# The first hidden tile of a streaming encoder: where ACT's squares, the norm row's copies and the first cached loads stand in their queues

## The chip, the cores and the metric

The kernel runs on one core of one Trainium2 chip. The metric is the device time of one execution in microseconds, the median over the runs shown. Traces come from the hardware profiler, one execution per kernel.

## What is computed

The reference is one inference step of a two-layer encoder for two groups of requests that share weights: a prompt group (512 new frames) and a sample group (64 frames of a running stream, with 1024 cached frames). Each layer is

```python
h = rmsnorm(x, norm_pre)                 # 1024 features per frame
cols_A, cols_B = split(h @ w_in)         # one combined input projection
x = x + rmsnorm(concat(silu(g_A) * A(h), silu(g_B) * B(h)) @ w_out, norm_post)
```

Layer 0 pairs multi-head latent attention (A) with stick-breaking attention (B); layer 1 pairs chunk-band attention with forgetting attention. The sample group's attention also reads cached keys and values. The change lies in the first microseconds of layer 0: `rmsnorm` of the input, its transposed copy, and the first 416 columns of `w_in` (the latents of A); and in the loads of the cached keys and values of B.

## The kernel before, in words

TensorE works in float32 split in two: every operand is kept as a rounded high part and a low part (the rest), and a product of two such operands is three matmuls (high x high, high x low, low x high).

The head of the kernel treats the input in five tiles: four of 128 prompt rows (tiles 0 to 3) and one of 64 sample rows (tile 4). Each tile is two halves of 512 features.

- `load_x` (L778) issues the two DMAs of a tile on SP's queue. `landed` (L159) makes a DMA wait, on its queue, until another DMA has landed; in the loop, tile 1's loads and the first two weight loads wait so for the first half of tile 0.
- `put_h` (L207) squares each half on ACT (L211, with the sum over the row read out), makes the reciprocal root on POOL (L197, L198), and scales the tile by it and by the norm row on DVE (L214).
- `put_hT` (L217) transposes a half with four PE transposes into one of two `psT` banks (L221), then ACT copies it as the high part of `hT` (L224) and DVE subtracts for the low part (L225).
- The norm row is one row of 1024 numbers. Two PE products with a column of ones spread it over 128 partitions into two `psA` banks (`nps`, L801). Tile 0 reads it there; ACT copies it into SBUF (`npre`, L809) for tiles 1 to 4.
- The weights of the first projection, eight slices k0 to k7 of 128 x 416, are loaded (`wraw`, four buffers), rounded to the high part on ACT (`chi`, L173), and their low part is made on POOL or, for k3 and k6, on DVE (L177). A load needs its `wraw` buffer back from the low part of the slice four before. In the loop, k0 and k1 follow tile 0; k2 to k5 tile 1; k6 and k7 tile 2.
- `tm_chunk` (L281) then makes the projection tile by tile: 24 matmuls of 128 x 128 by 416 columns into one of two `psA` banks (L270; L278 for the sample tile), three for each slice k, in the order k0 to k7. ACT copies the bank out (L854).
- After it come the pairs of heads of stick-breaking attention (`qk_pair`, L260 matmuls). `sb_sample` (L873) reads the cache in three chunks: `s_keys` (L530) loads 256 or 384 cached keys into `kraw` (two buffers) and `s_vals` (L544) the values into `vraw` (two buffers); ACT and POOL or DVE split them into high and low parts (L540, L541; L554, L555).

The order in which each engine and each queue gets its instructions isn't the program's: when the kernel is built, a planner simulates the engines and DMAs with estimated times, and at each moment gives a free engine the ready instruction of the best rank (program order, with a lead for the blocks under `tc.high_priority`). Each engine and each queue then runs its list strictly in that order on the chip. `tc.issue_after(ins)` makes the planner put the instructions of its block behind `ins` on `ins`'s engine, without a wait on a semaphore.

Of the kernel before, what the change touches and what calls it, by code (L numbers as in the profile page):

```python
# [1 line left out]

# [1 line left out]

# [9 lines left out]
AF = mybir.ActivationFunctionType  # L14
# [3 lines left out]
P = 128  # L18
# [41 lines left out]
def f32(ap):  # L60
    return ap.bitcast(F32)
# [3 lines left out]
def kernel(ctx: ExitStack, tc: tile.TileContext, a: dict, o: dict):  # L65
    nc = tc.nc
# [27 lines left out]
    def ring(shape, dt, tag, name=None):  # L94
        p, n = rings[tag]
        if isinstance(p, list):
            rings[tag][1] += 1
            return p[n % len(p)].tile(shape, dt, name=nm(name or tag), tag=tag, bufs=1)
        return p.tile(shape, dt, name=nm(name or tag), tag=tag, bufs=n)
# [4 lines left out]
    def Er(shape, name="e"):  # L104
        return ring(shape, F32, "E", name)
# [10 lines left out]
    def bank(tag, bufs, n=512):  # L116
        return lambda: pp.tile([P, n], F32, name=nm("ps" + tag), tag=tag, bufs=bufs)

    psA, psS, psT, psU, psX = bank("A", 2), bank("S", 2), bank("T", 2), bank("U", 1), bank("X", 1)
# [39 lines left out]
    def landed(dma, first):  # L159

        if first is not None:
            tc.add_manual_dep(dma.ins, first.ins.name,
                              mybir.DependencyInfo(mybir.DependencyClass.Sync, mybir.DependencyReason.DATA),
                              reason="landed")
        return dma
# [36 lines left out]
    ROOT = 1.0 / 32  # L202
# [1 line left out]
    def halves(x):  # L204
        return [x[:, :512], x[:, 512:]]

    def put_h(x, rows, npre, out):  # L207

        ss = St([P, 2])
        for c in range(2):  # L210
            nc.scalar.activation(psX()[:rows], x[c][:rows], AF.Square, scale=ROOT, accum_out=ss[:rows, c:c + 1])  # L211
        r = rstd_of2(ss, rows)
        for c in range(2):
            nc.vector.scalar_tensor_tensor(out=out[c][:rows], in0=x[c][:rows], scalar=r[:rows],  # L214
                                           in1=npre[c][:rows], op0=ALU.mult, op1=ALU.mult)

    def put_hT(x, rows, col, h):  # L217
        for g in range(2):
            t = psT().rearrange("p (a b) -> p a b", a=4)
            for k in range(4):  # L220
                nc.tensor.transpose(t[:, k, :rows], x[g][:rows, k * P:(k + 1) * P], ident[:rows, :rows])  # L221
            hi = h.m[g][:, :, 0, col:col + rows]
            lo = h.m[g][:, :, 1, col:col + rows]
            nc.scalar.copy(hi, t[:, :, :rows])  # L224
            nc.vector.tensor_sub(lo, t[:, :, :rows], f32(hi))  # L225
            if rows == DS:
                nc.vector.tensor_copy(out=h.s[g][:, :, 0:DS], in_=f32(hi))
                nc.vector.tensor_copy(out=h.s[g][:, :, DS:P], in_=f32(lo))

    def bcast(src_row, n):  # L230
        return bass.AP(src_row.tensor, src_row.offset, [[0, P], [1, n]])
# [78 lines left out]
    def drain():  # L310
        for _ in side[0]:
            pass
# [205 lines left out]
    def s_pv(po, ph, pl, vt, vnew, wd, first, last):  # L518
# [8 lines left out]
        for n, (l, r) in enumerate(ops):  # L527
            nc.tensor.matmul(po[:, :256], l, r, start=(first and n == 0), stop=(last and n == len(ops) - 1))  # L528

    def s_keys(kdram, c, new):  # L530

        k0, wd, nw = c
        raw = ring([P, 384], F32, "kraw")
        nc.sync.dma_start(raw[:, :wd], kdram[:, k0:k0 + wd])
        w = wd
        if nw:
            nc.gpsimd.tensor_copy(out=raw[:, wd:wd + nw], in_=new)
            w += nw
        kh, kl = ring([P, 384], F32R, "sK"), ring([P, 384], F32R, "sK")
        nc.scalar.copy(kh[:, :w], raw[:, :w])  # L540
        nc.gpsimd.tensor_sub(kl[:, :w], raw[:, :w], f32(kh[:, :w]))  # L541
        return kh, kl

    def s_vals(vdram, c, new):  # L544

        k0, wd, nw = c
        b0, nb = k0 // P, wd // P
        raw = ring([P, 3, P], F32, "vraw")
        nc.sync.dma_start(raw[:, :nb], vdram[:, b0:b0 + nb])
        v = ring([P, 3, 256], F32R, "vs")  # L550
        for dst, src in ((v[:, :nb], raw[:, :nb]),) + (((v[:DS, nb:nb + 1], new.unsqueeze(1)),) if nw else ()):
            src = src.rearrange("p a (s d) -> p a s d", s=2)
            hi = dst.rearrange("p a (s d) -> p a s d", s=4)[:, :, ::3, :]
            nc.scalar.copy(hi, src)  # L554
            nc.vector.tensor_sub(dst[:, :, 64:192].rearrange("p a (s d) -> p a s d", s=2), src, f32(hi))  # L555
        return v
# [217 lines left out]
    h0 = new_h(big)  # L774
# [3 lines left out]
    def load_x(t, first=None):  # L778
        rows = P if t < NT else DS
        x = [Rr([P, 512], "x") for _ in range(2)]  # L780
        ds = [landed(nc.sync.dma_start(f32(x[c][:rows]), xrow(t)[:, c * 512:(c + 1) * 512]), first) for c in range(2)]
        return [f32(y) for y in x], ds[0]
# [10 lines left out]
    x, first = load_x(0)  # L793
# [3 lines left out]
    nc.vector.memset(ones, 1.0)  # L797
    nps = []
    for c in range(2):
        nps.append(psA())  # L800
        nc.tensor.matmul(nps[c], ones, nrow[:, c * 512:(c + 1) * 512], start=True, stop=True)  # L801
    for t in range(NT + 1):
        rows = P if t < NT else DS
        put_h(x, rows, npre if t else nps, x)
        put_hT(x, rows, t * P, h0)
        if t == 0:
            npre = [Er([P, 512], "npre") for _ in range(2)]
            for c in range(2):
                nc.scalar.copy(npre[c], nps[c])  # L809

            nrm = Fr([P, 384], "nrm")
            for dst, src in ((rope, a["rope"]), (nrm[:, :256], bcast(a["a_q_norm"], 256)),
                             (nrm[:, 256:], bcast(a["a_kv_norm"], 128))):
                tc.keep_in_program_order(nc.scalar.dma_start(dst, src))
        if t < NT:
            c0_weights(C0W[t], first)
            x, _ = load_x(t + 1, first)
            first = None


# [74 lines left out]
    for p in range(NPAIR - 1):  # L895
        nxt = sb_qk(p + 1)
        if p == 1:
            v_chunk(sb, 1, a["w_vb"][1], h0, o["p_sbv"])
        if p == 1:
            tc.keep_in_program_order(nc.sync.dma_start(o["s_bandk"][:CL - DS], a["band_k"][DS:]))  # L900
            tc.keep_in_program_order(nc.sync.dma_start(o["s_bandv"][:CL - DS], a["band_vn"][DS:]))
        gate_tile(a["ws"][8 + p], h0, 4 + p, True)
        with tc.high_priority(PR_sb):
            beside(sb_sample(p), EV_sb)
            sb_pair(p, pr)
            drain()
        pr = nxt
    gate_tile(a["ws"][11], h0, 7, True)
    nc.sync.dma_start(o["s_sbv"], sb.vn)
# [179 lines left out]
    for c0 in range(0, PAST, 512):  # L1089
        raw = w_tile("wraw", [P, 512], F32)  # L1090
# [6 lines left out]
    t = psA()  # L1097
# [3 lines left out]
    for i in range(2):  # L1101
        raw = w_tile("wraw", [P, 512], F32)
# [6 lines left out]
    for i in range(2):  # L1109
        raw = w_tile("wraw", [P, 4, P], F32)  # L1110
# [68 lines left out]
    npre = l0.tile([P, D], F32, name="npre", tag="rq", bufs=1)  # L1179
# [164 lines left out]
    t = psT()  # L1344
    for i in range(NT):
        nc.tensor.transpose(t[:H, i * P:(i + 1) * P], lf[:, i, :], ident)
    c = Er([P, S], "cum")
# [3 lines left out]
    for k in range(3):  # L1351
        c = Er([P, 384], "cum")
# [3 lines left out]
    t = psT()  # L1356
# [191 lines left out]
```

## Time and profile before

| | |
|---|---|
| median of 3 runs | 833.12 us (832.88 to 835.7) |
| the profiled execution's own time | 829.8 us |
| its span, first to last instruction | 827.9 us |
| PE busy | 766.3 us (93% of the span), 5581 instructions |
| DVE, ACT, POOL busy | 507.6, 499.2, 382.6 us (61%, 60%, 46%) |
| the chain that ended last | PE 70%, DVE 10%, ACT 7%, DMA 5%, issue 4%, POOL 4% |
| DMA | 95.52 MB, mean 115 GB/s |

A busy time is the sum of an engine's instructions; matmuls overlap, so a busy PE isn't PE at its peak. The chain is followed back from the last instruction, at each step to what released it. In a timeline row the first number is the start in microseconds from the span's start, the second how long the merged instructions took, and the bracket at the end how long the engine was idle before, and what released it. "SPq" is SP's queue of DMA issues.

### The profile page before, as it was taken

Reading aid. Unit: us, or ns where it says so; the run is one execution under the profiler, and the core shown is the slowest. Engines: PE = TensorE matmul, PEld = TensorE weight load, DVE = VectorE, ACT = ScalarE, POOL = GpSimd, SP = SyncE. Lnnn points to the kernel's source line nnn. Section 1 sums busy time; section 2 is a strip of 40 time slices with the busy share of each in tenths; the row PEclk is TensorE's granted clock in tenths of the full one; section 3 lists DMA queues with packets and bytes.
Section 4 is the critical chain, followed back from the end, with each engine's and each line's share of the span. In section 5 each row is a group of like instructions: output and inputs, shape, how many; then the busy total and the mean of one; then the engine's idle time right before and its main releaser. Section 6 shows DMA issues by size and latency. Waiting matters only on the chain.

```text
span 827.9 us, 16285 instructions
## 1 busy us (share of the span) xinstructions
PE 766.3 (93%) x5581; PEld 713.1 (86%) x5581; DVE 507.6 (61%) x1318; ACT 499.2 (60%) x1342; POOL 382.6 (46%) x461
## 2 busy tenths in 40 slices
PE   6989999999997999989868999999997999999986
PEld 4989899989895888788767999999897899998986
DVE  4544765777847675738962654664754576658345
ACT  7554664776747675666542755575644767768521
POOL 7584342654427131055772644553344444546453
PEclk9999999999999999999998999999999999999999
DMA  8243324441123022146352443433223543551562
GB/s 271 60 145 114 101 73 146 142 122 53 54 68 109 29 73 74 40 139 218 122 171 72 123 118 104 136 110 99 87 81 111 170 127 111 158 140 55 158 228 102
DMA packets 69924, 95.52 MB, mean 115 GB/s; under 512 B 9529, under 2 KB 40489, under 8 KB 69810
## 3 DMA queue, kind: packets, MB, share of 16 engines
q1 hardware_dynamic: 69264, 94.12, 37.7%
q8 instruction: 44, 0.72, 0.4%
q14 instruction: 38, 0.31, 0.2%
q10 hardware_dynamic: 578, 0.37, 0.1%
HBM read 74.36 MB, written 18.79 MB: 113 GB/s over the span
## 4 chain that ended last, share of the span: by engine, by line
PE 70%; DVE 10%; ACT 7%; DMA 5%; issue 4%; POOL 4%; SPq 1%; DVEq 0%; POOLq 0%; ACTq 0%
PE psA L260 27%; PE psA L270 15%; PE psU L435 5%; PE psX L528 4%; PE psT L426 4%; PE psA L278 3%; PE psS L563 2%; PE psS L460 2%; PE psS L461 2%; POOL m L751 1%; DMA part<-part 1%; PE psT L509 1%; ACT whi L173 1%; DMA x<-in_x_prompt_dram 1%; PE psA L989 1%
## 5 line engine op out<-in xcount | busy, mean ns | idle before, releaser
L260 PE MATMUL psA<-hT,whi 128*128 128x320 f32 (+1 forms) x1216 | 258.5, 301 | 3.8 <-DVE foxqbl L353 2.0
L177 POOL TENSOR_TENSOR wlo<-wraw,whi 128x512 fp32r<-128x512 f32 (+2 forms) x130 | 168.6, 1307 | 188.4 <-ACT whi L173 146.2
L260 PEld LDWEIGHTS psA<-hT,whi 128*128 128x128 f32 x1216 | 198.8, 190 | 6.8 <-issue 2.7
L260 PE MATMUL psA<-hT,wlo 128*128 128x320 f32 (+1 forms) x608 | 183.5, 302 | 0.0
L270 PE MATMUL psA<-whi,hT 128*128 128x256 f32 (+2 forms) x812 | 162.8, 287 | 6.8 <-DVE m L745 5.5
L270 PEld LDWEIGHTS psA<-whi,hT 128*128 128x128 f32 x812 | 130.0, 188 | 9.5 <-DVE m L745 6.4
L270 PE MATMUL psA<-wlo,hT 128*128 128x256 f32 (+2 forms) x420 | 121.2, 288 | 0.0
L260 PEld LDWEIGHTS psA<-hT,wlo 128*128 128x128 f32 x608 | 115.8, 190 | 0.8
L173 ACT CAST whi<-wraw 128x512 fp32r<-128x512 f32 (+2 forms) x130 | 78.2, 616 | 39.8 <-PE psA L260 21.4
L270 PEld LDWEIGHTS psA<-wlo,hT 128*128 128x128 f32 x420 | 79.5, 189 | 0.8
L371 POOL TENSOR_TENSOR kz<-kf,r 64x256 fp32r<-64x256 f32 x48 | 36.7, 765 | 30.5 <-ACT kf L365 28.8
L430 DVE TENSOR_TENSOR pt1l<-psT,pt1h 128x384 fp32r<-128x384 f32 x64 | 39.6, 620 | 14.6 <-ACT pt1h L429 13.7
L1237 DVE CUSTOM_DVE_ANT_0 x<-psS,T 128x128 f32<-128x128 f32 (+1 forms) x64 | 31.0, 484 | 23.0 <-PE psT L426 8.5
L447 POOL TENSOR_TENSOR g<-g,oT 128x512 f32<-128x512 f32 x14 | 18.3, 1304 | 53.8 <-DVE oT L439 53.5
L541 POOL TENSOR_TENSOR sK<-kraw,sK 128x384 fp32r<-128x384 f32 (+2 forms) x32 | 30.3, 946 | 26.3 <-ACT sK L540 24.6
L469 ACT ACTIVATE psS<-x,st 128x128 f32<-128x128 f32 (+1 forms) x64 | 34.1, 532 | 13.8 <-DVE st L1237 13.5
L429 ACT CAST pt1h<-psT 128x384 fp32r<-128x384 f32 x64 | 33.9, 531 | 12.6 <-PE psT L426 11.7
L528 PE MATMUL psX<-vs,sP 128*128 128x256 f32 (+1 forms) x184 | 38.6, 303 | 1.5 <-DVE sP L515 1.2
L439 DVE SCALAR_TENSOR_TENSOR oT<-psU,oT 64x256 f32<-64x256 f32 x64 | 26.8, 419 | 18.6 <-ACT oT L438 17.7
L460 PE MATMUL psS<-r,r 128*128 128x256 f32 (+1 forms) x96 | 35.4, 370 | 2.6 <-DVE st L1237 1.7
L347 ACT ACTIVATE r<-psA 64x256 fp32r<-64x256 f32 x48 | 18.2, 378 | 32.4 <-PE psA L260 16.9
L472 DVE TENSOR_SCALAR x<-psS,st 128x128 f32<-128x128 f32 (+1 forms) x64 | 35.1, 548 | 1.3
(390 smaller groups left out, 1893.9 us busy)
## 6 DMA issues: line engine op xcount, KB each, us to landing
wraw<-in_ws_dram SPq DMA_DIRECT2D x80, 256.0 KB
wraw<-in_w_out_dram SPq DMA_DIRECT2D x32, 256.0 KB
x<-in_x_prompt_dram SPq DMA_DIRECT2D x16, 256.0 KB
part<-part SPq DMA_DIRECT2D x32, 128.0 KB
m<-part SPq DMA_DIRECT2D x16, 256.0 KB
r<-r SPq DMA_DIRECT2D x48, 64.0 KB
out_dram<-kout SPq DMA_DIRECT2D x12, 256.0 KB
out_dram<-vf SPq DMA_DIRECT2D x24, 128.0 KB
```

The lines of the kernel that those rows point to most:

```text
L173: nc.scalar.copy(hi, raw)
L177: eng.tensor_sub(lo, raw, f32(hi))
L260: nc.tensor.matmul(ps[:, :c1 - c0], w[:, k % 4, :], h.m[k // 4][:, k % 4, x, c0:c1], start=(k == 0 and n == 0), stop=(k == KT - 1 and n == 2))
L270: nc.tensor.matmul(ps[:, :n], h.m[k // 4][:, k % 4, x, t * P:(t + 1) * P], w[:, k % kp, :], start=(k == ks[0] and m == 0), stop=(k == ks[- ...
L371: nc.gpsimd.tensor_sub(pair.kl[s][me, cs], kf[me, cs], f32(k[me, cs]))
L429: nc.scalar.copy(ph[:, :i + 1, at], tv)
L430: nc.vector.tensor_sub(pl[:, :i + 1, at], tv, f32(ph[:, :i + 1, at]))
L435: nc.tensor.matmul(po, m.v[p // 2, j][:, p % 2, s * P:(s + 1) * P], x[:, j, :], start=(j == 0 and x is ph), stop=(j == 2 * hq + 1 and x is ...
L460: nc.tensor.matmul(ps[:, :w], pair.qq[s][:, q], pair.kk[s][:, :w], start=True, stop=False)
L469: nc.scalar.activation(ps[:, :n], src, AF.Exp, bias=mn, scale=-1.0, accum_out=sm)
L472: nc.vector.tensor_scalar(out=w[:, :n], in0=ps[:, :n], scalar1=rs, scalar2=None, op0=ALU.mult)
L528: nc.tensor.matmul(po[:, :256], l, r, start=(first and n == 0), stop=(last and n == len(ops) - 1))
```

## The change

Three edits. The norm row's two products go to `psS` banks and no longer to `psA`. On ACT, the squares of tile 1 and the two copies of the norm row are put behind the last transposed copy of tile 0 (the second half's L224). The DMAs of cached keys and values of the first pair of heads (`lead[0]` is set while the head runs and cleared after the first pair's pass) wait on SP's queue until the first half of the input tile loaded last, the sample tile, has landed.

```diff
--- before.py
+++ after.py
@@ -1,4 +1,4 @@
-from contextlib import ExitStack
+from contextlib import ExitStack, nullcontext
 
 import numpy as np
 
@@ -204,11 +204,12 @@
     def halves(x):
         return [x[:, :512], x[:, 512:]]
 
-    def put_h(x, rows, npre, out):
+    def put_h(x, rows, npre, out, behind=None):
 
         ss = St([P, 2])
-        for c in range(2):
-            nc.scalar.activation(psX()[:rows], x[c][:rows], AF.Square, scale=ROOT, accum_out=ss[:rows, c:c + 1])
+        with tc.issue_after(behind.ins) if behind else nullcontext():
+            for c in range(2):
+                nc.scalar.activation(psX()[:rows], x[c][:rows], AF.Square, scale=ROOT, accum_out=ss[:rows, c:c + 1])
         r = rstd_of2(ss, rows)
         for c in range(2):
             nc.vector.scalar_tensor_tensor(out=out[c][:rows], in0=x[c][:rows], scalar=r[:rows],
@@ -221,11 +222,12 @@
                 nc.tensor.transpose(t[:, k, :rows], x[g][:rows, k * P:(k + 1) * P], ident[:rows, :rows])
             hi = h.m[g][:, :, 0, col:col + rows]
             lo = h.m[g][:, :, 1, col:col + rows]
-            nc.scalar.copy(hi, t[:, :, :rows])
+            done = nc.scalar.copy(hi, t[:, :, :rows])
             nc.vector.tensor_sub(lo, t[:, :, :rows], f32(hi))
             if rows == DS:
                 nc.vector.tensor_copy(out=h.s[g][:, :, 0:DS], in_=f32(hi))
                 nc.vector.tensor_copy(out=h.s[g][:, :, DS:P], in_=f32(lo))
+        return done
 
     def bcast(src_row, n):
         return bass.AP(src_row.tensor, src_row.offset, [[0, P], [1, n]])
@@ -527,11 +529,13 @@
         for n, (l, r) in enumerate(ops):
             nc.tensor.matmul(po[:, :256], l, r, start=(first and n == 0), stop=(last and n == len(ops) - 1))
 
+    lead = [None]
+
     def s_keys(kdram, c, new):
 
         k0, wd, nw = c
         raw = ring([P, 384], F32, "kraw")
-        nc.sync.dma_start(raw[:, :wd], kdram[:, k0:k0 + wd])
+        landed(nc.sync.dma_start(raw[:, :wd], kdram[:, k0:k0 + wd]), lead[0])
         w = wd
         if nw:
             nc.gpsimd.tensor_copy(out=raw[:, wd:wd + nw], in_=new)
@@ -546,7 +550,7 @@
         k0, wd, nw = c
         b0, nb = k0 // P, wd // P
         raw = ring([P, 3, P], F32, "vraw")
-        nc.sync.dma_start(raw[:, :nb], vdram[:, b0:b0 + nb])
+        landed(nc.sync.dma_start(raw[:, :nb], vdram[:, b0:b0 + nb]), lead[0])
         v = ring([P, 3, 256], F32R, "vs")
         for dst, src in ((v[:, :nb], raw[:, :nb]),) + (((v[:DS, nb:nb + 1], new.unsqueeze(1)),) if nw else ()):
             src = src.rearrange("p a (s d) -> p a s d", s=2)
@@ -797,16 +801,18 @@
     nc.vector.memset(ones, 1.0)
     nps = []
     for c in range(2):
-        nps.append(psA())
+        nps.append(psS())
         nc.tensor.matmul(nps[c], ones, nrow[:, c * 512:(c + 1) * 512], start=True, stop=True)
     for t in range(NT + 1):
         rows = P if t < NT else DS
-        put_h(x, rows, npre if t else nps, x)
-        put_hT(x, rows, t * P, h0)
+        put_h(x, rows, npre if t else nps, x, behind if t == 1 else None)
+        done = put_hT(x, rows, t * P, h0)
         if t == 0:
+            behind = done
             npre = [Er([P, 512], "npre") for _ in range(2)]
-            for c in range(2):
-                nc.scalar.copy(npre[c], nps[c])
+            with tc.issue_after(behind.ins):
+                for c in range(2):
+                    nc.scalar.copy(npre[c], nps[c])
 
             nrm = Fr([P, 384], "nrm")
             for dst, src in ((rope, a["rope"]), (nrm[:, :256], bcast(a["a_q_norm"], 256)),
@@ -814,7 +820,7 @@
                 tc.keep_in_program_order(nc.scalar.dma_start(dst, src))
         if t < NT:
             c0_weights(C0W[t], first)
-            x, _ = load_x(t + 1, first)
+            x, lead[0] = load_x(t + 1, first)
             first = None
 
 
@@ -904,6 +910,7 @@
             beside(sb_sample(p), EV_sb)
             sb_pair(p, pr)
             drain()
+        lead[0] = None
         pr = nxt
     gate_tile(a["ws"][11], h0, 7, True)
     nc.sync.dma_start(o["s_sbv"], sb.vn)
```

## Rows read from the trace of the kernel before

**Rows 1.** Windows: stretch, length; busy PE, PEld, DVE, ACT, POOL; clock, DMA share, GB/s.
```profile
10.00:11.00 1.00, 0.00 (x0) 0.00 (x0) 0.00 (x0) 1.00 (x4) 0.31 (x2) 1.00 1.00 386
14.00:20.00 6.00, 6.00 (x30) 5.80 (x29) 4.80 (x8) 5.12 (x14) 4.83 (x6) 1.00 1.03 278
40.00:52.00 12.00, 11.07 (x85) 10.70 (x84) 7.28 (x13) 8.06 (x23) 11.39 (x16) 1.00 0.47 138
60.00:828.00 768.00, 715.80 (x5294) 668.30 (x5293) 476.33 (x1255) 462.27 (x1245) 339.37 (x377) 0.98 0.37 112
```

**Rows 2.** Windows of line L270 alone: PE, PEld, clock, DMA share, GB/s.
```profile
14.40:16.30 1.90, 1.87 (x5) 1.51 (x5) 1.00 1.04 218
26.60:31.20 4.60, 4.60 (x26) 4.54 (x25) 1.00 0.11 25
```

**Rows 3.** Timeline of PE in the head.
```profile
7.16 1.97 PE L221 MATMUL psT<-ident,x 128*128 128x128 f32 x8 [1.13 <-DVE x L214]
11.52 0.72 PE L270 MATMUL psA<-chi,hT 128*128 128x416 f32 x1 [2.40 <-ACT hT L224]
...
13.67 1.12 PE L221 MATMUL psT<-ident,x 128*128 128x128 f32 x4 [1.08 <-DVE hT L225]
...
16.32 0.69 PE L221 MATMUL psT<-ident,x 128*128 128x128 f32 x4
...
22.54 0.63 PE L270 MATMUL psA<-chi,hT 128*128 128x416 f32 x2
```

**Rows 4.** Timeline of ACT in the head.
```profile
8.04 0.60 ACT L211 ACTIVATE psX<-x 128x512 f32<-128x512 f32 x1 [0.92 <-DMA x<-in_x_prompt_dram]
...
8.67 0.56 ACT L809 COPY npre<-psA 128x512 f32<-128x512 f32 x1
9.79 0.60 ACT L211 ACTIVATE psX<-x 128x512 f32<-128x512 f32 x1 [0.55 <-DMA x<-in_x_prompt_dram]
...
10.88 1.07 ACT L224 CAST hT<-psT 128x512 fp32r<-128x512 f32 x2
...
11.85 0.98 ACT L173 CAST chi<-wraw 128x416 fp32r<-128x416 f32 x2
...
16.62 0.60 ACT L211 ACTIVATE psX<-x 128x512 f32<-128x512 f32 x1 [0.55 <-DMA x<-in_x_prompt_dram]
...
17.67 0.41 ACT L554 CAST vs<-vraw 128x256 fp32r<-128x256 f32 x1 [0.33 <-DMA vraw<-in_sb_v_dram]
...
18.46 0.54 ACT L173 CAST chi<-wraw 128x416 fp32r<-128x416 f32 x1
```

**Rows 5.** Timeline of DVE in the head.
```profile
11.60 1.41 DVE L214 SCALAR_TENSOR_TENSOR x<-x,st,npre 128x512 f32<-128x512 f32 x2 [3.83 <-POOL st L198]
12.93 1.28 DVE L225 TENSOR_TENSOR hT<-psT,hT 128x512 fp32r<-128x512 f32 x2
14.13 1.36 DVE L177 TENSOR_TENSOR wlo<-wraw,chi 128x416 fp32r<-128x416 f32 x1
...
19.64 2.23 DVE L214 SCALAR_TENSOR_TENSOR x<-x,st,npre 128x512 f32<-128x512 f32 x2
21.80 0.58 DVE L177 TENSOR_TENSOR whi<-wraw,chi 128x416 fp32r<-128x416 f32 x1
```

**Rows 6.** Timeline of POOL in the head.
```profile
12.47 2.56 POOL L177 TENSOR_TENSOR wlo<-wraw,chi 128x416 fp32r<-128x416 f32 x2 [0.91 <-ACT chi L173]
...
20.13 1.19 POOL L177 TENSOR_TENSOR whi<-wraw,chi 128x416 fp32r<-128x416 f32 x1 [0.93 <-ACT chi L173]
```

**Rows 7.** Timeline of SP's queue: issue times of three loads.
```profile
1.63 0.43 SPq L534 DMA_DIRECT2D kraw<-in_sb_kT_dram  x1
3.47 0.80 SPq L168 DMA_DIRECT2D wraw<-in_w_c_dram  x2
...
14.68 1.16 SPq L168 DMA_DIRECT2D wraw<-in_w_c_dram  x2
```

**Rows 8.** Line L540 in the first 200 us: the splits of cached keys.
```profile
L540 ACT CAST sK<-kraw x11: 459/501/517, 59.3 to 196.8; 128x384 fp32r<-128x384 f32 x7, 128x320 fp32r<-128x320 f32 x4
```

## The prediction

> **What bounds the kernel now.** I read the windows by stretch first. From 60 us to the end PE is busy 715.8 of 768 us [rows 1]: it is the bound there, with 52.2 us of idle time in all, and nothing of the change works there directly. The head is another matter: between 10 and 11 us PE does nothing while ACT is busy all the time and the DMA engines are full (share 1.00, 386 GB/s) [rows 1]. So I read PE's timeline of the head for what it waits for. Tile 0's eight transposes run at 7.16 and end at 9.13; then PE idles 2.40 us until the first projection product at 11.52, released by ACT's copy L224, and 1.08 us more until tile 1's transposes at 13.67, released by DVE's L225 [rows 3]. ACT's timeline shows why the copy came late: at 8.04 and 9.79 ACT stood at the head of its queue for the two halves of tile 1 to land (0.92 and 0.55 us idle), squared them, copied the norm row (0.56 each), and only at 10.88 ran tile 0's two copies, ready since 9.13 [rows 4]. DVE then scaled tile 1 first (11.60) and made tile 0's low parts at 12.93 [rows 5]. From 13.67 on PE has work without a break, but not from plenty: the products of slice k6 start at 22.54, right after DVE's low part of k6 (21.80, 0.58 us) [rows 3, 5]. From then on products follow each other every 0.18 us (26 in 4.60) [rows 2].
>
> **The change part by part.** The sum is made on the profiled execution (829.8 us, span 827.9, 1.9 us around it), which lies 3.3 us below the median 833.12; differences are carried over to the median as they are.
>
> 1. Tile 0's copies ahead of the squares and the norm row. The same ten ACT instructions run, none added. The second transposed half is there at 9.13 and a copy takes about 0.55 (1.07 for two), so both are done at 9.7 in place of 11.95 [rows 3, 4]. ACT was idle for 1.47 us in two pieces before 9.79; now it is idle before each of the copies, about as long, so ACT as a whole gains nothing: it only does another thing first. DVE, idle 3.83 us before 11.60, can take the two low parts (1.28) by about 10.4 in place of 14.2 [rows 5].
>
> 2. What PE does with it. The three products each of k0 and k1 can run between 8.9 and 11.5, where before two ran; four products are then ahead of their old place. In this stretch a product took 0.38 us (five in 1.90), later 0.18; both windows list a granted clock of 1.00, so the trace does not say by that column why [rows 2]. Four products are worth 1.5 us at the one pace and 0.7 at the other.
>
> 3. What it costs tile 1. Its second half lands at 9.79 at the earliest [rows 4]. The squares now start behind the second copy, at 9.7, and take 0.73 each with the read-out; they end at 11.2, or at 12.3 if the planner puts both norm-row copies (1.1) before them; before it was 10.5. So tile 1's scaling slides from 11.60 to 12.3 to 13.4, and the first transposes of tile 1 come at 13.0 to 14.1 where 13.67 is the old time: they had waited for a psT bank that DVE held, and that wait is gone. This part lies between a gain of 0.7 and a loss of 0.4; I take 0. The norm row's copies themselves are needed only by that scaling.
>
> 4. The feed of later slices. PE's lead lasts only if k6 and k7 come earlier too. Their loads are issued at 14.68 and about 15.5 [rows 7], when slices k2 (POOL, from 12.47) and k3 (DVE, 14.13 to 15.49) give their buffers back [rows 5, 6]. ACT's casts of k2 and k3 stood at 11.85; they move to between 10.3 and 12.4 (behind the copies, before or behind squares and norm row), so k6's load moves by -1.5 to +0.6. DVE has 1.28 us less to do after 11.60, and loses the first value split out of the stretch as well: ACT's L554 (0.41, after 0.33 of waiting) stood just ahead of k6's cast at 18.46 [rows 4]. DVE's low part of k6 at 21.80 can so come about 1.3 to 1.7 us earlier; if the order on DVE does not favour it, nothing. I take 1.5, as the nearest row is DVE's own 1.28 with the split's share on top.
>
> 5. The cached loads. kraw's issue at 1.63 goes; SP then issues nothing until 3.47, when tile 0 has landed, so SP gains nothing [rows 7]. Its 128 KB (128 partitions of 256 keys of four bytes) are at 386 GB/s 0.34 us of the DMA engines; between tile 0 and the weights these were not full, so 0 to 0.3, and I take 0. The keys are first split at 59.3 [rows 8], so a landing at 18 to 20 us is early enough by about 40. Nothing waits for them that early. The new wait stands on SP's queue, and every load behind it waits too: this is the second rival.
>
> 6. The norm row in psS. The two psA banks are free from the start; the first product waited for ACT's copy, not for a bank [rows 3]. psS is used only by the attention, much later: 0.
>
> Sum: the smaller of PE's lead (0.7 to 1.5) and the feed's (0 to 1.7) decides; I take 1.5 us for both, with 0 and 3.8 (the whole move of the low parts) as ends. Behind 22.54 PE is the bound without a break up to 40 us, and in the stretch from 40 to 52, where it idles 0.93 us of 12 and POOL is at 11.39 [rows 1], POOL's work starts with buffers that the end of the projection frees, so it moves along. The gain should arrive at the end: span 826.4, its execution 828.3, the median **831.6 us**. About 0.5%, 4.2 us, is what can be told from no change; this is 0.2%.
>
> A rule of the Trainium skill speaks against part 3, and a row bears on it first: DVE's two scalings took 1.41 us at 11.60 but 2.23 at 19.64, where POOL ran a subtraction at 20.13 [rows 5, 6]. The page "SBUF — State Buffer", section "Who interferes with whom", has it that a DVE instruction with two SBUF inputs contends with a GpSimd instruction that reads SBUF. L214 with npre is such an instruction, and the trace agrees as far as that pair goes. By it the moved scaling of tile 1 would be slowed by POOL; without it the sum stays as above.
>
> **The rivals.**
>
> - *The rest is ordered anew.* The planner lays out the whole kernel from its own simulated times. Another head can give other orders on DVE, ACT and PE far behind it, for better or worse. For: the lists come from one simulation, and the head's loads and splits change places. Against: behind the head all moves alike. Its size: PE's idle time after 60 us is 52.2 us [rows 1]; a tenth of it, 5.2, as an estimate, beside the 1.5: 826.4 to 836.8.
> - *SP stands still (slower).* If the planner puts the key and value loads ahead of k6's, they wait on the queue for the sample tile. Tile 3's second half was used at 16.62, when it landed, and the values issued behind the sample tile at 17.67 [rows 4], so the sample tile lands at about 17.1. With one to four issues of 0.43 ahead [rows 7], k6 is issued at 17.5 to 18.8 in place of 14.68. It took at most 3.8 us from issue to its cast; with 3, a cast of 0.54 and a low part of 0.58 to 1.19 [rows 4 to 6], k6 is ready at 21.6 to 23.5 and k7 about 0.9 later, against 22.4 before. PE loses up to 2 us in place of its gain: about 834.6, slower. It decides from the point where a key load stands ahead of k6's load on SP. For it: before, a value load did stand between the sample tile's and k6's. Against: those loads had no wait then, and the planner fills a queue with what is ready.
> - *Tile 1 pays.* Its scaling moves to 12.3 to 13.4, beside POOL's pair at 12.47 (2.56 us) [rows 6]; the slow pair cost 0.82 more than the other (2.23 less 1.41) [rows 5]. With the 0.4 of part 3, and the low parts of k2 and k4 held up as long, the lead is eaten: 832.9.
> - *The whole lead holds.* All of the 3.8 us by which tile 0's low parts come earlier is passed on, as k2 to k7 each move up: 829.3. Against it: ACT is busy 5.12 of 6 us from 14 to 20 and the DMA engines are full there [rows 1], and neither has less to do before 16 us.
>
> **How the numbers follow.** Forecast 0.34; new order 0.34 (0.18 faster by over 0.5%, 0.05 within, 0.11 slower); SP stands still 0.14 (0.10 within, 0.04 slower); tile 1 pays 0.08; whole lead 0.10 (half of it past the bound). Faster 0.18 + 0.05 = 0.23; within 0.34 + 0.05 + 0.10 + 0.08 + 0.05 = 0.62; slower 0.11 + 0.04 = 0.15. The range runs from 826.5 to 836.5, the new order's ends but for its outermost cases; the forecast's own is 829.3 to 833.1.
>
> **What would show it.** ACT's timeline: L224 of tile 0 at 8.2 and 9.2, the squares and the norm row behind. PE: first product near 9, no idle 2.40 us under L224; the stretch in front of tile 1's transposes. DVE: L225 before L214 of tile 1. Products of k6 at about 21 in place of 22.54, and the first L260 product about 1.5 us earlier than before. SP's queue: where L534 and L549 stand, and whether k6's load waits behind them. The forecast is wrong if k6 starts no earlier, if the first L260 product moves by another amount than the end does (then a later order changed), or if the time leaves 829 to 833.

## The result, and the profile after

The changed kernel took 842.05 us (median of 4 runs, 841.17 to 842.49) against 833.0 us for the kernel before (4 runs, 831.56 to 835.7): ratio 1.0094, 95% interval 1.0071 to 1.0116. It is slower by about 0.9%, where 831.6 us and "no change" were forecast, and 842.05 lies outside the range. The profiled execution took 842.49 us with a span of 840.4.

The windows of the changed kernel, in the columns of [rows 1]; the last two stretches are new.

```profile
14.00:20.00 6.00, 5.15 (x17) 3.21 (x15) 0.84 (x2) 4.49 (x12) 3.61 (x5) 1.00 0.95 274
40.00:52.00 12.00, 12.00 (x82) 11.51 (x81) 6.87 (x14) 5.53 (x14) 8.26 (x14) 1.00 0.21 57
60.00:828.00 768.00, 721.72 (x5300) 672.30 (x5300) 471.85 (x1249) 464.54 (x1252) 342.21 (x382) 0.98 0.37 112
24.00:30.00 6.00, 5.83 (x19) 4.96 (x19) 4.76 (x9) 3.86 (x13) 3.61 (x7) 0.50 0.05 14
68.00:74.00 6.00, 5.61 (x26) 5.61 (x27) 0.00 (x0) 1.04 (x4) 1.91 (x4) 0.50 0.46 137
```

In the head DVE, busy 4.80 of 6 us before, has 0.84, and PE starts 17 products and transposes in place of 30. From 24 to 30 us the granted clock is 0.50, the lower of its two levels (1.2 of 2.4 GHz), and again from 68 to 74; before, both stretches were at 1.00.

PE's timeline of the same head (start, length, idle before and its releaser), against [rows 3]:

```profile
6.79 1.97 PE L222 MATMUL psT<-ident,x 128*128 128x128 f32 x8 [0.75 <-DVE x L215]
11.27 0.72 PE L272 MATMUL psA<-chi,hT 128*128 128x416 f32 x1 [2.50 <-ACT hT L225]
...
20.21 0.35 PE L272 MATMUL psA<-chi,hT 128*128 128x416 f32 x1
21.54 1.30 PE L222 MATMUL psT<-ident,x 128*128 128x128 f32 x8 [0.98 <-DVE x L215]
23.56 0.71 PE L272 MATMUL psA<-chi,hT 128*128 128x416 f32 x1 [0.72 <-ACT hT L225]
```

The first product comes 0.25 us earlier, not 2.5. Then PE does all 24 of tile 0's products alone, waits for slices between them, and meets tile 1 only at 21.54, where before its transposes ran at 13.67 and 16.32. ACT's timeline says why (ACTq are the issues of transfers on ACT's own queue), against [rows 4]:

```profile
10.19 0.54 ACT L173 CAST chi<-wraw 128x416 fp32r<-128x416 f32 x1 [3.11 <-DMA wraw<-in_w_c_dram]
10.63 0.58 ACT L225 CAST hT<-psT 128x512 fp32r<-128x512 f32 x1
10.74 0.36 ACTq L820 DMA_DIRECT2D rope_qf<-in_rope_dram  x1
...
12.08 0.34 ACTq L820 DMA_DIRECT2D nrm<-in_a_q_norm_dram  x1
...
13.47 0.33 ACTq L820 DMA_DIRECT2D nrm<-in_a_kv_norm_dram  x1
13.91 0.60 ACT L212 ACTIVATE psX<-x 128x512 f32<-128x512 f32 x1 [0.79 <-DMA wraw<-in_w_c_dram]
...
15.40 0.59 ACT L212 ACTIVATE psX<-x 128x512 f32<-128x512 f32 x1
```

Ahead of tile 0's first copy the planner now has the cast of slice k2, and ACT stands 3.11 us for that slice to land. Behind it come the copies, the norm row's copies and the three small transfers (rope and two norm rows), which before stood at 9.89, 10.29 and 11.47, behind or beside tile 1's squares. Tile 1's first square runs at 13.91, 4.1 us behind the time at which its second half was squared before. POOL's list adds to it (against [rows 6]):

```profile
15.14 1.07 POOL L177 TENSOR_TENSOR wlo<-wraw,chi 128x416 fp32r<-128x416 f32 x1 [3.26 <-ACT chi L173]
16.17 1.07 POOL L177 TENSOR_TENSOR whi<-wraw,chi 128x416 fp32r<-128x416 f32 x1
17.33 0.30 POOL L197 TENSOR_SCALAR st<-st 128x1 f32<-128x1 f32 x1
18.79 1.07 POOL L177 TENSOR_TENSOR whi<-wraw,chi 128x416 fp32r<-128x416 f32 x1 [1.16 <-ACT chi L173]
19.82 0.79 POOL L198 TENSOR_TENSOR st<-st,mhalf 128x1 f32<-128x1 f32 x1
```

The low part of k7 stands between the two steps of tile 1's root (L197, L198) and waits for its slice; so the root is done at 20.6, where before it ran at 10.99. DVE, against [rows 5]:

```profile
17.91 0.59 DVE L177 TENSOR_TENSOR whi<-wraw,chi 128x416 fp32r<-128x416 f32 x1 [4.87 <-ACT chi L173]
...
20.64 1.42 DVE L215 SCALAR_TENSOR_TENSOR x<-x,st,npre 128x512 f32<-128x512 f32 x2 [0.46 <-POOL st L198]
```

Tile 1 is scaled at 20.64 in place of 11.60 [rows 5]. SP's queue, against [rows 7], has the loads of k6 and k7 at 11.90, ahead of the first keys:

```profile
11.90 1.11 SPq L168 DMA_DIRECT2D wraw<-in_w_c_dram  x2
...
15.95 0.34 SPq L538 DMA_DIRECT2D kraw<-in_sb_kT_dram  x1
```

How late the changed kernel is, product by product of PE against the same product of the kernel before: 0.4 us early below 10 us, 6.8 late at 34 to 42, 13.2 at 64 to 90, 11.6 from 110 to 200 and 12.4 at the end. So little is lost behind 110 us. Not all of this is the change's: the profiled execution of the kernel before (829.8 us) is at the fast end of its own, which in the comparisons below lay between 829.9 and 837.6.

### The profile page after: what moved, and what is told of

Same layout as the page of the kernel before. It is cut to its first block, busy times and chain, and to the rows that moved or that the text cites. A ratio compares the mean times of both kernels' runs of the same rounds, so it can differ in the third digit from the quotient of the medians.

```text
span 840.4 us, 16278 instructions
## 1 busy us (share of the span) xinstructions
PE 776.3 (92%) x5581; PEld 718.2 (85%) x5581; DVE 507.7 (60%) x1318; ACT 499.6 (59%) x1342; POOL 380.8 (45%) x461
## 4 chain that ended last, share of the span: by engine, by line
PE 66%; DVE 9%; ACT 8%; issue 3%; POOL 3%; DMA 3%; SPq 1%; DVEq 0%; POOLq 0%; ACTq 0%
PE psA L262 26%; PE psA L272 14%; PE psU L437 5%; PE psX L530 4%; PE psT L428 4%; PE psA L280 2%; PE psS L567 2%; PE psS L462 2%; PE psS L463 1%; ACT whi L173 1%; PE psT L511 1%; DMA m<-part 1%; DVE m L758 1%; PE psA L996 1%; POOL m L755 1%
## 5 line engine op out<-in xcount | busy, mean ns | idle before, releaser
L272 PE MATMUL psA<-whi,hT 128*128 128x256 f32 (+2 forms) x812 | 165.4, 291 | 7.0 <-DVE m L749 4.2
L272 PEld LDWEIGHTS psA<-whi,hT 128*128 128x128 f32 x812 | 132.2, 192 | 10.5 <-DVE m L749 5.3
L272 PE MATMUL psA<-wlo,hT 128*128 128x256 f32 (+2 forms) x420 | 124.0, 295 | 0.1
L272 PEld LDWEIGHTS psA<-wlo,hT 128*128 128x128 f32 x420 | 81.9, 195 | 1.6 <-POOL wlo L177 0.6
L471 ACT ACTIVATE psS<-x,st 128x128 f32<-128x128 f32 (+1 forms) x64 | 34.1, 533 | 13.7 <-DVE st L1244 13.5
L440 ACT ACTIVATE oT<-psU 64x256 f32<-64x256 f32 x64 | 24.3, 379 | 21.3 <-PE psU L437 20.1
```

The source lines that it names most:

```text
L272: nc.tensor.matmul(ps[:, :n], h.m[k // 4][:, k % 4, x, t * P:(t + 1) * P], w[:, k % kp, :], start=(k == ks[0] and m == 0), stop=(k == ks[- ...
L471: nc.scalar.activation(ps[:, :n], src, AF.Exp, bias=mn, scale=-1.0, accum_out=sm)
```

## The experiments

"Late at" is the median distance of PE's products from the same products of the kernel before in the two profiled executions, by the time before. "At 0.50" is PE's time at the lower granted clock from 6 to 44 and from 44 to 90 us of the run's own time, added up from windows of 1 us. The traces' records of the clock begin at 16.49 us (before), 16.56 (changed) and 10.36 to 19.99 (e1 to e15); ahead of the first record a window reads 1.00, but a product starts 0.35 us after the last one, as in stretches at 0.50, and not 0.19 as from the first record on at 1.00. So the column for the head leaves out the lower pace ahead of the record.

| kernel | median us | ratio, 95% interval | late at 34–42 | 64–90 | 110–200 | at 0.50 |
|---|---|---|---|---|---|---|
| before | 833.0 to 835.1 | | 0 | 0 | 0 | 0, 0 |
| changed | 842.05 | 1.0094, 1.0071–1.0116 | 6.8 | 13.2 | 11.6 | 6.8, 10.2 |
| e1 loads only | 838.58 | 1.0067, 1.0034–1.0099 | 2.1 | 5.8 | 5.8 | 0, 3.4 |
| e2 ACT edits only | 844.58 | 1.0124, 1.0085–1.0162 | 7.4 | 12.3 | 10.7 | 6.8, 6.8 |
| e3 + root first | 842.78 | 1.0100, 1.0085–1.0115 | 6.8 | 10.1 | 8.6 | 6.8, 3.4 |
| e4 before, root late | 838.18 | 1.0045, 1.0030–1.0060 | 3.2 | 6.7 | 5.1 | 0, 3.4 |
| e5 e3 + issues behind | 842.28 | 1.0078, 1.0043–1.0113 | 8.8 | 12.5 | 11.0 | 13.7, 3.4 |
| e6 before, ACT's pair order | 836.0 | 1.0030, 1.0008–1.0051 | 0.3 | 4.0 | 2.4 | 0, 6.8 |
| e7 changed, ACT's pair order | 844.44 | 1.0113, 1.0079–1.0147 | 4.9 | 9.3 | 7.7 | 0, 3.4 |
| e8 e5 + ACT's pair order | 844.39 | 1.0107, 1.0077–1.0138 | 6.7 | 14.9 | 13.3 | 10.2, 13.7 |
| e9 e3 + issues first | 836.6 | 1.0019, 1.0000–1.0039 | 1.3 | 4.9 | 3.3 | 0, 3.4 |
| e10 changed + issues first | 840.23 | 1.0071, 1.0044–1.0099 | 2.5 | 7.4 | 7.3 | 3.4, 6.8 |
| e11 before, DVE's pair order | 837.22 | 1.0032, 1.0012–1.0052 | 0.0 | 4.6 | 3.0 | 0, 6.8 |
| e12 changed + filler | 845.52 | 1.0131, 1.0098–1.0164 | 8.0 | 11.7 | 10.2 | 3.4, 3.4 |
| e13 e10 + old pair order | 838.64 | 1.0043, 1.0028–1.0057 | 3.4 | 5.3 | 3.7 | 3.4, 0 |
| e14 e9 + old pair order | 838.18 | 1.0045, 1.0027–1.0063 | 1.4 | 4.7 | 4.8 | 6.8, 3.4 |
| e15 changed + old pair order | 844.64 | 1.0112, 1.0094–1.0131 | 5.4 | 8.7 | 7.1 | 3.4, 3.4 |

**Which part of the change.** e1 keeps the wait of the cached loads alone, e2 the edits on ACT with the norm row in psS.

```diff
 e1: the kernel before, and
+        landed(nc.sync.dma_start(raw[:, :wd], ...), lead[0])   # keys and values
 e2: the changed kernel, but
+        landed(nc.sync.dma_start(raw[:, :wd], ...), None)
```

> Of the change only the cached loads' wait: squares, norm row and its banks as before. Theory 'late root' (the changed kernel loses because tile 1's squares on ACT and above all its reciprocal root on POOL came to stand behind the splits of k4, k5 and k7, so that tile 1's scaling ran at 20.6 us in place of 11.6): here the root of tile 1 stands where it stood before, ahead of k2's low part on POOL, so about as before, 830 to 836 us, and the first L26x product of the pairs at 39 to 42 us. Theory 'loads' (the loads that wait for the sample tile hold up SP's queue): the loss is here, 839 to 845. Theory 'luck of the new order' (any edit of the head gives another order far behind it): anything, and offsets against before that change again and again after 100 us.

> The squares of tile 1 and the norm row's copies behind tile 0's copies, norm row in psS, but no wait of the cached loads. 'Late root': POOL's list has tile 1's root behind k7's low part as in the changed kernel, so 838 to 845 us, tile 1's scaling at 18 to 21 us and the pairs' first product at 45 to 48. 'Loads': as before, 830 to 835.

The ACT edits alone lose as much as the whole change (1.0124 against 1.0094, the intervals overlap). The loads' wait alone costs 1.0067, and its 838.58 us lies between the ranges named for it: the squares of tile 1 stay early, but the lists shift by some tenths, and tile 1's scaling, which starts at 11.81, then runs beside POOL's low part of k2 at 11.73 and takes 2.21 us in place of 1.41. That is 0.8 of the 2.1 us in the head; the start of the scaling is 0.2 more, and the rest was not traced to a wait.

**Why tile 1 is late in the head.** e3 puts POOL's low parts of k2 to k5 behind tile 1's root, and ACT's casts of them behind tile 1's squares. e4 does the opposite to the kernel before: tile 1's root stands behind the low part of k5 on POOL. For that the loads and splits of k2 to k5 stand ahead of tile 1's step in the program, and ACT's list changes with them.

```diff
 e3: e2, and in split(), for slices 2 to 5
+        with tc.issue_after(squares_of_tile_1.ins): nc.scalar.copy(hi, raw)
+        with tc.issue_after(root_of_tile_1.ins):    eng.tensor_sub(lo, raw, f32(hi))
 e4: the kernel before, and in tile 1's step
+        c0_weights(C0W[1])                          # from behind put_hT() to ahead of put_h()
+        with tc.issue_after(low_part_of_k5.ins):    r = rstd_of2(ss, rows)
```

> As the second kernel, but the casts of k2 to k5 on ACT are put behind tile 1's squares and their low parts on POOL behind tile 1's root; nothing else. 'Late root': the loss goes, tile 1's scaling runs at 12 to 14 us and the time falls to 828 to 835. If the copies ahead of the squares are themselves the loss (tile 1 later by 1 to 2 us, norm row, psS), it stays over 837.

> The kernel before, with the root of tile 1 put behind the low part of k5 on POOL (the splits of k2 to k5 ahead of tile 1 in the program); squares, norm row and loads as before. 'Late root': POOL's order alone makes the loss, tile 1's scaling at 16 to 19 us and 836 to 842 us. If ACT's order of copies and squares makes it, about as before, 831 to 835.

e4: a late root, with the order that comes with it, costs 3.2 us in the head; tile 1's scaling comes at 18.10. But in e3, where the root is first, the head is as late as in the changed kernel. ACT's timeline of e3:

```profile
11.51 0.36 ACTq L829 DMA_DIRECT2D rope_qf<-in_rope_dram  x1
12.87 0.34 ACTq L829 DMA_DIRECT2D nrm<-in_a_q_norm_dram  x1
14.14 0.33 ACTq L829 DMA_DIRECT2D nrm<-in_a_kv_norm_dram  x1
14.57 0.60 ACT L219 ACTIVATE psX<-x 128x512 f32<-128x512 f32 x1 [3.71 <-DMA wraw<-in_w_c_dram]
```

Tile 0's copies now run at 8.45 and 9.30, as forecast, and then ACT stands 3.71 us. Each of the three issues comes about 1.3 us behind the one before it: in the program each waits until an earlier transfer of its completion counter has landed (the eight counters are used in turn by SP's loads and these), and what stands behind it on ACT waits too. The first, at 11.51, came when a weight load issued at 6.20 had landed. e5 and e9 move only these issues, behind the squares and to the start.

```diff
 e5: e3, with the three issues moved into tile 1's step
+        with tc.issue_after(squares_of_tile_1.ins): dma = nc.scalar.dma_start(dst, src)
 e9: e3, with the three issues moved ahead of the loop over the tiles
+    for dst, src in (rope, q norm, kv norm): tc.keep_in_program_order(nc.scalar.dma_start(dst, src))
+    for t in range(NT + 1):
```

> The kernel of 'ACT edits alone, tile 1's chain first' with one thing moved: the three DMA issues on ACT's queue (rope and the two norm rows) are issued behind tile 1's second square instead of ahead of the first. Theory (the three issues, each waiting for a DMA lane, held ACT for 3.71 us and with it tile 1): tile 1's first square starts by 11.2 us, its scaling by 13.5, PE's idle of 5.03 us ahead of tile 1 shrinks below 2 us, the products of tile 0 and 1 stand at -0.5 to +1.5 us against the kernel before at 30 us, and with the +3.5 us of the first pair's stage the run ends at 833 to 837. Rival (tile 1 is late for another reason, POOL's and ACT's lists): the head stays at +4 to +7 and the run at 840 to 844.

> The kernel of 'three DMA issues behind tile 1's squares' with those issues moved the other way: to the start, behind the first slice's copy, where the lanes they take over have long landed. Theory (an issue that waits for a DMA lane holds ACT, whichever side of the squares it stands on): no wait over 0.6 us at the three issues; tile 1's scaling at 12.5 to 13.8 us; the copy of slice 2 starts below 13.5 us and not at 16.74; the products stand at -1 to +1.5 us against the kernel before at 40 us. Rival (the lead itself costs, since PE runs out of slices and its clock falls): +3 to +6 at 40 us. The end is 3.5 us above what stands at 40 us if the first pair's stage keeps its other order.

In e5 tile 1 is scaled at 13.31, so the issues had held it; but the hold only moved, to what is now behind them:

```profile
16.36 0.33 ACTq L823 DMA_DIRECT2D nrm<-in_a_kv_norm_dram  x1
16.74 1.86 ACT L178 CAST chi<-wraw 128x416 fp32r<-128x416 f32 x4 [4.51 <-DMA x<-in_x_sample_dram]
```

All four casts wait until 16.74, PE idles, its clock stands at 0.50 for 13.7 us of the head, and the expected 833 to 837 us failed (842.28). e9 is the counter-test (ACT's rows, then PE's first product and DVE's scaling of tile 1):

```profile
6.40 0.36 ACTq L816 DMA_DIRECT2D rope_qf<-in_rope_dram  x1
...
7.41 0.33 ACTq L816 DMA_DIRECT2D nrm<-in_a_kv_norm_dram  x1
...
10.77 0.64 ACT L219 ACTIVATE psX<-x 128x512 f32<-128x512 f32 x1
...
12.18 0.96 ACT L178 CAST chi<-wraw 128x416 fp32r<-128x416 f32 x2
...
9.05 0.71 PE L279 MATMUL psA<-chi,hT 128*128 128x416 f32 x1
...
13.35 3.02 DVE L222 SCALAR_TENSOR_TENSOR x<-x,st,npre 128x512 f32<-128x512 f32 x2 [2.71 <-POOL st L204]
```

No hold is left, and the head is 1.3 us late in place of 6.8 (e3): one edit of three lines, 836.6 us in place of 842.78. PE's waits from 6 to 40 us sum to 3.8 us in e9 and to 4.6 in the kernel before, so this order does save PE about 0.8 us of waiting. But a product takes 0.35 us until 19.9 in e9, and until 16.3 before. Half of those 3.6 us, about 1.8, is an estimate of what that costs, and the two make 1.0 of the 1.3 us. The same edit on the changed kernel:

```diff
 e10: the changed kernel, with the three issues moved ahead of the loop as in e9
```

> The changed kernel with that one edit, the three DMA issues at the start, and no other fence. Theory: ACT reaches tile 1's first square 0.7 to 1.4 us earlier than the 13.91 us of the changed kernel, but POOL's list still has the low parts of slices 2, 4 and 5 ahead of tile 1's root, so its scaling stays behind 17 us and the head at +3 to +6.5 us; the run ends at 837.5 to 842. Rival (the three issues are the whole cause): scaling below 14 us, the head within 1 us of before.

In e10, ACT's second square of tile 1, the last step of its root, and POOL's low part of k5:

```profile
14.21 0.62 ACT L212 ACTIVATE psX<-x 128x512 f32<-128x512 f32 x1
15.95 0.57 POOL L198 TENSOR_TENSOR st<-st,mhalf 128x1 f32<-128x1 f32 x1
17.04 1.20 POOL L177 TENSOR_TENSOR whi<-wraw,chi 128x416 fp32r<-128x416 f32 x1 [0.52 <-ACT chi L173]
```

Of the changed kernel's 6.8 us in the head 2.5 are left, fewer than the 3 to 6.5 expected. Tile 1's first square is at 13.16, its scaling at 16.55, earlier than the 17 us expected, since POOL's root no longer had k5 and k7 ahead of it. So moving three small transfers on ACT's queue gives back 4.3 us of the 6.8. ACT's hold by itself is the smaller part of that: tile 1's second square starts 1.2 us earlier (14.21, not 15.40), but the last step of its root 3.9 us earlier (15.95, not 19.82), because the planner, given the other place of the issues, also ordered POOL's list anew. The runs don't part the two here; e3 and e9, where POOL has the root first in both, show the hold without that. The lists of ACT and POOL make about 1.2 us more (e9 against e10, which differ in the loads' wait as well).

**Whether PE's idle time makes the half clock.** e12 adds 13 products, that repeat finished ones into a spare bank, to the changed kernel.

```diff
 e12: in tm_prompt(), tile 0, behind slices 5, 6, 7
+    for _ in range((4, 4, 5)[k - 5]):
+        mm = nc.tensor.matmul(spare[:, :n], h.m[k // 4][:, k % 4, 0, :P], hi[:, k % kp, :], start=True, stop=True)
```

> The changed kernel with 13 extra products into a spare bank behind tile 0's last three slices (they repeat a product that is done, nothing reads them), in PE's idle stretches of 17.5 to 21.5 us. All engines' lists are otherwise those of the changed kernel in this stage. Theory (PE's idle time ahead of tile 1 is why its granted clock is 0.50 from 23.4 to 30.2 us, and that costs about half of the head's loss): clock 1.00 from 23 to 31 us, tile 1's first product still at 23 to 24 us, +3 to +4.5 us at 35 us instead of +6.8, the end 2 to 4 us earlier than the changed kernel. Rival (the clock falls for another reason): 0.50 again over 6.8 us and +6.5 to +8 us at 35 us.

Inconclusive: the planner also put ACT's copy of tile 1 later, its first product came at 25.81 in place of 23.56 after another 2.88 us of idle time, and the clock stood at 0.50 behind that (3.4 us, in place of 6.8). What the runs do show is an order of events: in the changed kernel 0.50 begins at 23.4, behind an idle stretch of PE of 0.98 us and within one of 0.72, in e5 at 14.1, at the end of one of 2.98. But not each idle stretch is followed by it: e7 and e15 run the changed kernel's lists in the head, and there PE was 0 and 3.4 us at 0.50, with 4.9 and 5.4 us of delay in place of 6.8. So some 1.9 us of the head go with the recorded stretch at 0.50, which did not come in every execution, and about 5 us do not. Those are longer waits of PE and the lower pace ahead of the clock's first record, and the runs don't divide them.

**The first pair's stage (42 to 60 us).** From the head to 64–90 us the changed kernel loses another 6.4 us, e1 to e5 each 3.3 to 4.9. I had two theories of order: ACT copies the first key bank ahead of q's second sample piece (e6 puts that order into the kernel before, e7 and e8 take it out of the changed kernel and of e5), or DVE scales tile 3's latent keys ahead of q's first small low part (e11 puts it into the kernel before, e13 to e15 take it out of e10, e9 and the changed kernel, with ACT's order too).

```diff
 e6: the kernel before, in k_cb() of the first pair, first half
+        with tc.high_priority(200): nc.scalar.copy(pair.kk[s][me, cs], ...); nc.scalar.copy(kf[:, cs], ...)
 e7, e8: the changed kernel, e5; there
+        with tc.issue_after(pair.qb.ins): ...     # behind q's second sample piece
 e11: the kernel before, in q_cb() of the first pair
+        with tc.issue_after(scaled_keys_of_tile_3.ins): (the first low part, qbl)
 e13, e14, e15: e10, e9, the changed kernel; latents(3) and latents(4) traced behind q, their scaling behind qbl, and e7's edit
```

> The kernel before with one edit at 42 to 50 us: ACT copies the first pair's first key bank (the two halves and kf) ahead of q's second sample piece, as in every variant so far; the head is not touched. Theory (the +3.5 us of the first pair's stage come from that order by itself): the same product stands at 0 before 42 us and at +2.5 to +4.5 us from 60 us on, the run ends 2.5 to 4.5 us above the kernel before. Rival (the order is only a mark of a late head, whose loss the stage shows later): 0 to +0.5 us at 60 and at the end.

> The changed kernel with the first pair's old order put back: q's second sample piece is copied ahead of the second half of the first key bank and of kf. Theory (that order costs 3.5 us by itself): +6.8 us at 42 us as in the changed kernel, but no further loss to 60 us, and the run ends at 837.5 to 840. Rival (order without a price): +10 at 60 us and 841 to 843 as before.

> Both mends together on the ACT edits: tile 1's chain ahead of the slices' copies, the three DMA issues behind tile 1's squares, and the first pair's old order. Theory (the loss is made of these two orders): -1 to +1.5 us at 30 and at 60 us, the run ends at 830 to 835, within 0.3% of the kernel before. Rival (the edits themselves cost): 837 or more.

> The kernel before with one edit in the first pair's stage: VectorE scales tile 3's latent keys (128x128) ahead of the first of q's two small low parts, as in every variant so far. The head is not touched. Theory (VectorE's order, not ACT's, makes the loss of 42 to 60 us: that scaling waits for POOL's root and took 1.36 us in the changed kernel, and ACT's next copy waits behind it): 0 at 45 us, +2 to +3.7 us at 56 us and from there on, the run 2 to 4 us above the kernel before. Rival (the stage's loss is the late head's in another form): 0 to +0.7 us.

> The changed kernel with the three DMA issues at the start and, in the first pair's stage, VectorE's scaling of tile 3's latent keys behind q's first small low part, as the kernel before has it. Theory (the two orders are separate parts of the loss): the head at +2 to +3.5 us at 40 us as with the issues at the start alone, then no step between 46 and 58 us (below 0.7 us outside stretches at half clock), where that kernel and the changed one lose 3 to 3.5 us; the run ends at 836 to 839. Rival (the stage loses it in another wait): +2.5 us or more between 46 and 58 us again.

> The ACT edits, tile 1's chain first, the three DMA issues at the start and the first pair's old order. Theory: +1 to +1.5 us at 40 us as with the same kernel without the last mend, and the same at 60 us; the run ends 0 to 2 us above the kernel before, 834 to 837. Rival (the stage loses it in another wait): 838 or more.

> The changed kernel with the first pair's old order alone. Theory: +6.8 us at 40 us as in the changed kernel, no step between 46 and 58 us of it, the run ends at 838 to 840.5. Rival: another 3 us lost there, 841 to 843.

PE's waits from 46 us to the end of this stage (total, times, longest), first the kernel before:

```profile
PE psA L382 <- ACT kf L365: 1.1, 1, 1.1
PE psA L260 <- DVE sbqbl L353: 0.7, 1, 0.7
PE psA L270 <- ACT kout L384: 0.6, 1, 0.6
PE psT L847 <- DVE lat L836: 0.2, 1, 0.2
```

The changed kernel:

```profile
PE psA L262 <- ACT kf L367: 1.8, 1, 1.8
PE psA L384 <- ACT kf L367: 1.4, 1, 1.4
PE psT L853 <- DVE lat L842: 0.6, 1, 0.6
PE psA L272 <- ACT kout L386: 0.6, 1, 0.6
```

And e13:

```profile
PE psA L262 <- DVE sbqbl L356: 1.5, 1, 1.5
PE psA L390 <- ACT kf L371: 1.4, 1, 1.4
PE psT L860 <- DVE lat L849: 0.7, 1, 0.7
PE psA L272 <- ACT kout L392: 0.6, 1, 0.6
```

The waits sum to 2.6, 4.4 and 4.2 us. Beside them only the clock is left, and the two give the whole: the waits beyond 2.6, and half of the time at 0.50, make 1.8 + 5.1 = 6.9 us for the changed kernel (6.4 measured), 1.8 + 1.7 = 3.5 for e9 (3.6), 1.2 + 3.4 = 4.6 for e11 (4.6; its waits sum to 3.8) and 1.6 + 0 for e13 (1.9). In the other twelve kernels the same sum comes within 0.5 us of the measured loss, but for e8 (9.1 against 8.2).

ACT's order is not the cause: e6 is 0.3 us late at 34 to 42 and still 0.3 in the median of 50 to 60. The rest of its 4.0 goes with 0.7 us more of waits (3.3 in sum) and 6.8 us at 0.50, and taking the order out in e7 left more waits (4.8) and not fewer. DVE's order is a small one: it adds 1.2 us of waits in e11, whose time came as expected (2.1 us above the kernel before), but with the clock's help. Taking it out gave back 0.1 in e13 (4.2, and 4.3 in e10): the wait went from kf to DVE's low part, which was the rival named there. e13 lost less in this stage because no stretch at 0.50 followed; e14 and e15, with the same lists there, had 3.4 us of it and lost 3.3. So my reading of a loss of 3.5 us by order failed; it was about 1.8 us of waits and the clock behind them. What makes the rest of the waits stays open, and so does why the clock fell there in every profiled kernel but the one before and e13.

No version beat the kernel before; e9 comes nearest.

## Why the prediction was wrong

The mechanism behind the change was right, and e3, e5 and e9 show it by itself: tile 0's copies can run at 8.4 and 9.3 us, and the first product at 9.05 (e9). In the changed kernel that did not happen, and where it did, no gain reached the end. Two terms failed: what else runs ahead of the copies (part 1), and the 0 us for tile 1 (part 3).

- **Part 1 failed first.** "The same ten ACT instructions run ... it only does another thing first" took the rest of ACT's list as fixed. The planner put slice k2's cast ahead of the first copy, and its wait for the slice took 3.11 us; the copies came at 10.63 and 11.55, not at 8.2 and 9.2. I counted instructions and left out what else could slip ahead of a copy that the edit does not hold in its place.
- **Part 3 is the term that was mis-sized, and it decides the time.** I let tile 1's scaling slide from 11.60 to 12.3 to 13.4 and took 0 us. It slid to 20.64. The three transfers on ACT's queue, which I nowhere counted, now stand ahead of the squares (moving them gave back 4.3 us of the head in e10, with POOL's list ordered anew by it); POOL's list has low parts ahead of the root and between its steps (3.2 us in e4). With both mended, the casts of k2 to k5 behind the squares and without the loads' wait, the scaling stands at 13.35 (e9), in the forecast's slide. What I weighed on DVE beside POOL shows there as well: 3.02 us for the two scalings of e9 with two of POOL's low parts beside them, 1.41 without [rows 5]. This agrees with the rule of the Trainium skill ("SBUF — State Buffer", "Who interferes with whom") that the prediction names.
- **Part 2.** PE's lead is there in e9 and is nearly all given back: after k0 and k1 it waits 1.05 us for k2 and 1.58 for tile 1, and about 0.8 us of waiting is saved in all. The pace that [rows 2] left open, 0.38 us a product beside a clock of 1.00, lies ahead of the clock's first record at 16.49, and there 1.00 tells nothing. In e9 that pace lasted until 19.9. In the changed kernel the lead turned into PE's doing tile 0 alone.
- **Part 4 was right in direction.** The low part of k6 came at 17.91 in place of 21.80, 3.9 us earlier and not 1.5, but tile 1 was not there to use it. I named the feed as the limit; the limit was tile 1.
- **Part 5** ("0") missed that the same wait reorders the head: e1 loses 2.1 us there, 0.8 of them for the reason of "Tile 1 pays", DVE beside POOL. That rival had the right price (0.82), but in the changed kernel the scaling took 1.42: its sum of 832.9 had tile 1 late by 0.4, not by 9 us.
- **The rivals.** "SP stands still" did not occur: k6 and k7 are issued at 11.90, the keys at 15.95. "The rest is ordered anew" was the right kind of case, but I sized it by PE's idle time behind 60 us and kept the head out of it. The loss sits in the head and the stage right behind it; behind 110 us the changed kernel's distance goes up and down (10.9 to 14.0 in medians of 5 us) and ends at 12.4. Its slower cases were priced without a row on ACT's own queue, which the edit moves past the squares.

## What to carry to other kernels

An edit that only says "behind X" fixes a lower bound: list again every instruction of that engine that becomes ready in the gap, transfers on its queue first, since an issue that must wait for its counter stops the engine's arithmetic behind it (3.71 us in e3, 4.51 in e5, no such wait in e9). Such issues belong where the transfers whose counters they reuse have long landed. And when a stage runs two tiles interleaved, the price of a lead is the delay of the other tile, not the engine's busy time.

## What was not expected of the hardware

- The time of one program follows PE's granted clock: over 68 executions of the kernel before, 829.9 to 837.6 us at mean granted clocks of 0.988 to 0.976, a straight line through them falls by 0.53 us for each 0.001, with a correlation of -0.73. So 2.5 us between two profiled executions, alone, show nothing.
- The granted clock falls from 1.00 to 0.50 in single stretches in all of these runs. In the changed kernel they add up to 38.8 us within the span, in the kernel before's profile to 26.4. By half of the 12.4 us between them, some 6 of the 12.4 us at the end are clock, an estimate from these two sums.
- The clock's records begin only at 10.36 to 19.99 us, and ahead of the first one products keep the lower pace while a window reads 1.00. e3 and e9 run PE's list alike up to 11 us, and their first records stand at 11.28 and 19.99.
